# Weights laid out by the host in reading order, gates kept in the tokens' order, and a new order of the work

## The chip, the cores and the metric

The kernel runs on one core of a Trainium2 chip. Such a core has a matrix engine (PE; its weight loads are listed apart as PEld), a vector engine (DVE), a scalar engine (ACT), a GpSimd engine (POOL) and a sync engine (SP), which here issues the DMAs. The metric is the device time of one execution in microseconds (us), as the median of several runs.

## The reference

Two sequences of 512 tokens with 1024 features (`x_prompt`, `x_sample`) pass through the same two layers. Layer 1 is differential attention, layer 2 retention in both directions. Both project to queries, keys, values and a gate of 2048 columns, and multiply the mixer's output by the gate's SiLU before the output projection.

```python
h = rms_norm(x, norm_g[i], NORM_EPS)
proj = h @ w_in                                   # (512, 1024) @ (1024, 8192 or 6144)
q, k, v, gate = jnp.split(proj, [...], axis=-1)
# layer 1: rotary halves; a = softmax(q1 k1) - lam * softmax(q2 k2); o = a @ v
# layer 2: rotation of even and odd columns; retention forward plus backward
o = rms_norm(o, subln_g, SUBLN_EPS)               # layer 1: times 1 - lambda_init
o = o.reshape(B, S, D_INNER) * jax.nn.silu(gate)
x = x + o @ w_out                                 # (512, 2048) @ (2048, 1024)
```

A last `rms_norm` closes the trunk. All of it is float32.

## The kernel before

**Products.** Each float32 operand is split into two parts, a high part (a cast, `hi_of`, line 496, on ACT) and the rest (a subtraction, `lo_of`, line 499, on DVE), and a product takes three passes on PE (`PASSES`). A projection of 256 columns is a `Unit`: its 1024 x 256 block of weights is loaded as two tiles of 512 KB (`raw`, four buffers), split into `ws` tiles (seven buffers), and multiplied by a scheme of seven half-size products, P1 to P7, in place of eight. Sums of weight blocks (line 667, `st` tiles) and sums of the transposed input (line 573, `m` tiles, split into `b` tiles by lines 496 and 499) feed them; products come out in the banks `pj`, `sc` and `o` (`tp` serves transposes), and `evac` copies a bank to a `c` tile on ACT (line 775) or adds a bank and a `c` tile into an `e` tile on DVE (line 783). There are four `c` and eight `e` buffers.

**The token order.** PE reads the input with tokens woven (tokens a and a + 256 side by side), so outputs of a unit come out in woven order. A gate unit (`gate_done`) takes the tanh (line 879, into the `c` tile that its sum has used up), forms (1 + tanh) x (line 886, into the `e` tile; for the first head line 882, in two halves, which puts the tokens in order), scales it (line 888) and stores it to DRAM (`g`, 256 KB). Weights of wide units (values) and of the output projection are woven while they are split: the two instructions read and write a 128 x 1024 tile in steps of two elements.

**Later use.** `load_sg` loads the gate again, and `weigh` (line 969) multiplies the mixer's output by it into another `c` tile, `og`, reading the woven gate in steps of two. `og` is split (lines 496, 499), and the sum of its squares is transposed (line 982) for the norm.

**What sets the order.** `Plan.op` records every operation with a cost and its predecessors, `arrange` places the operations on the engines by a list schedule in order of due times, and `issue` then adds random shifts to the due times of operations near the times in the table `SHIFTS` (time, span back, size, share, seed), a row at a time. The result is one fixed program per engine, each engine working strictly in its own order. All loads and stores go through SP's queue (line 492) in the program's order. A tile can be written again only when the last reader or store of its buffer is done. In this program the last use of a gate's `c` buffer is line 886 and that of its `e` buffer is the store.

Of the kernel before, what the change touches and what calls it, by code (L numbers as in the profile page):

```python
# [13 lines left out]
ALU = mybir.AluOpType  # L14
# [68 lines left out]
def unwoven_rows(t):  # L83
    return t.rearrange("p k (b a) -> p k a b", a=2)


def flat_unwoven_rows(t):
    return t.rearrange("p k (a b) -> p k a b", a=2)


class Buf:
# [22 lines left out]
    (11.25, 30, 4, 0.5, 330243),  # L114
    (621.17, 30, 0.3, 0.5, 683747),
    (617.17, 30, 4, 1, 573989),
    (9.22, 4, 0.3, 0.5, 209685),
    (983.72, 4, 1, 0.5, 4667),
    (619.77, 4, 2, 0.5, 822278),
    (981.05, 4, 4, 0.5, 73582),  # L120
    (993.13, 30, 2, 1, 330152),
    (38.58, 16, 2, 1, 882644),
    (992.0, 4, 4, 1, 27528),
    (982.44, 30, 1, 1, 197187),
    (69.81, 8, 4, 1, 506276),
    (71.79, 16, 4, 0.05, 134658),
    (50.47, 30, 2, 0.05, 359379),
    (14.98, 16, 4, 0.2, 753457),
    (10.72, 30, 2, 0.2, 157696),
    (7.22, 8, 2, 0.2, 458750),  # L130
# [201 lines left out]
def trunk_kernel(  # L332
# [289 lines left out]
    class Unit:  # L622
        def __init__(self, w, c0, kind, done, view=None, weave=woven):
# [3 lines left out]
            self.view = view or (lambda r, i: r[:, :, i * P:(i + 1) * P])  # L627
# [8 lines left out]
        def take(self, i, k):  # L636

            if (i, k) not in self.x:
                c0 = self.c0 + (256 * i if self.wide else 0)
                r = slot(self.early + k, [P, 4, 256], F32) if self.early is not None else raw_t([P, 4, 256])  # L640
                src = self.w[k * S:(k + 1) * S, c0:c0 + 256].rearrange("(k p) c -> p k c", p=P)
# [5 lines left out]
                if self.wide:  # L647
                    self.x[i, k] = ((lambda: r.t), r)
                else:
                    for n in range(2):  # L650
                        self.x[n, k] = ((lambda n=n: self.view(r.t, n)), r)
            return self.x[i, k]

        def like(self, t):

            if self.wide or len(self.x[0, 0][0]().shape) == 3:
                return t
            return t.rearrange("p k (j i) -> p k j i", j=2)

        def prep(self, op):  # L660
# [3 lines left out]
            def combine(a, b, fn):  # L664
                t = st_t([P, 4, n])
                out = ((lambda: self.like(t.t)), t)
# [22 lines left out]
            if op == "P1" and self is first_units[0]:  # L689
                for k in range(2):  # L690
                    ks = slice(2 * k, 2 * k + 2)
                    hi_of(2 * n, lambda ks=ks: self.like(hi[0]())[:, ks], lambda ks=ks: src[0]()[:, ks],
                          [(src[1], n) for n in (2 * k, 2 * k + 1)], [(s, (0, k))])
                    lo_of(2 * n, lambda ks=ks: self.like(lo[0]())[:, ks], lambda ks=ks: src[0]()[:, ks],
                          lambda ks=ks: self.like(hi[0]())[:, ks],
# [1084 lines left out]
```

## Time and profile before

| | |
|---|---|
| median of 3 runs | 1723.61 us (1723.57 to 1723.65) |
| the profiled execution | 1725.69 us, with a span of 1723.9 us from the first to the last instruction |
| mean granted clock of PE in the span | 0.999 |
| PE, DVE, ACT, POOL busy | 1709.6, 1500.4, 935.1, 127.9 us |
| bytes moved | 328.82 MB, of it 209.55 MB read from HBM |
| busiest DMA queue (SP's) | 55.7% of 16 engines |

The table's busy times are averages over stages with different limits. A row of the trace gives the start, the duration, the engine, the line of the program, output and input, and in brackets the idle time ahead of it with what ended it. Rows carry the names that the program gives to its tiles: `arena` is one large buffer for inputs, queries, keys and values, `pad` holds small columns.

### The profile page before, as it was taken

The numbers are of one execution on the slowest core, as the hardware profiler recorded it, in microseconds if no ns is written. First come the engines' busy times: TensorE is split into PE (matmuls) and PEld (weight loads), VectorE is DVE, ScalarE is ACT, GpSimd is POOL, SyncE is SP. The second block draws the span as 40 slices with busy tenths as digits, with TensorE's granted clock in tenths as the row PEclk, the third lists the DMA queues.
The fourth block names the chain that finished last, engine by engine and source line by source line (L and its number), as shares of the span: only waits on it lengthen the run. The fifth ranks groups of instructions, "written<-read, shape, count | busy, mean of one in ns | idle before, by whom it ended". The sixth has DMA issues, their size and how long they took to land.

```text
span 1723.9 us, 27813 instructions
## 1 busy us (share of the span) xinstructions
PE 1709.6 (99%) x10317; PEld 1558.3 (90%) x10317; DVE 1500.4 (87%) x2406; ACT 935.1 (54%) x1864; POOL 127.9 (7%) x256
## 2 busy tenths in 40 slices
PE   9999999999999999999999999999999999999998
PEld 7889989999988889999999988898999998999997
DVE  8978888788699889988888898888898977999988
ACT  8754454444444665555555877555545464544446
POOL 1000000000000012111111200000000000111114
PEclk9999999999999999999999999999999999999999
DMA  6345546564545695555454525475747569665652
GB/s 228 127 159 149 172 151 185 173 193 136 186 135 177 225 357 192 196 196 195 160 201 142 196 68 166 138 217 171 225 138 249 156 211 410 255 250 198 247 205 98
DMA packets 162816, 328.82 MB, mean 191 GB/s; under 512 B 12772, under 2 KB 76920, under 8 KB 162680
## 3 DMA queue, kind: packets, MB, share of 16 engines
q1 hardware_dynamic: 162352, 326.71, 55.7%
q8 instruction: 81, 1.33, 0.3%
q14 instruction: 55, 0.45, 0.1%
q10 hardware_dynamic: 328, 0.34, 0.1%
HBM read 209.55 MB, written 117.44 MB: 190 GB/s over the span
## 4 chain that ended last, share of the span: by engine, by line
PE 92%; DVE 4%; ACT 1%; DMA 1%; issue 1%; POOL 0%; SPq 0%; POOLq 0%; DVEq 0%; ACTq 0%
PE pj L722 20%; PE pj L1060 18%; PE sc L722 11%; PE pj L732 10%; PE o L722 8%; PE sc L732 5%; PE o L1395 5%; PE sc L1334 5%; PE o L732 2%; PE o L1605 2%; PE sc L1560 1%; PE tp L1584 1%; PE o L1613 1%; PE pj L1375 1%; PE tp L1375 1%; DVE ws L499 1%
## 5 line engine op out<-in xcount | busy, mean ns | idle before, releaser
L1060 PE MATMUL pj<-ws,arena 128*128 128x512 f32 x1542 | 358.2, 380 | 0.0
L1060 PEld LDWEIGHTS pj<-ws,arena 128*128 128x128 f32 x1542 | 283.9, 189 | 36.2
L722 PE MATMUL pj<-b,ws 128*128 128x512 f32 x1080 | 251.4, 380 | 0.3 <-DVE b L499 0.3
L722 PEld LDWEIGHTS pj<-b,ws 128*128 128x128 f32 x1080 | 202.5, 189 | 28.5 <-DVE b L499 0.7
L1066 DVE SCALAR_TENSOR_TENSOR b<-pj,pad,b 128x512 f32<-128x512 f32 (+1 forms) x257 | 190.6, 743 | 12.4 <-PE pj L1060 11.8
L496 ACT CAST ws<-st 128x512 fp32r<-128x512 f32 (+1 forms) x192 | 140.4, 738 | 101.3 <-PE pj L722 28.5
L499 DVE TENSOR_TENSOR ws<-raw,ws 128x512 fp32r<-128x512 f32 (+2 forms) x165 | 153.2, 932 | 44.8 <-ACT ws L496 42.7
L496 ACT CAST ws<-raw 128x512 fp32r<-128x512 f32 (+2 forms) x165 | 153.6, 936 | 66.9 <-PE o L722 35.4
L499 DVE TENSOR_TENSOR ws<-st,ws 128x512 fp32r<-128x512 f32 (+1 forms) x192 | 151.6, 795 | 39.9 <-ACT ws L496 37.3
L722 PE MATMUL sc<-arena,ws 128*128 128x512 f32 x768 | 176.9, 379 | 0.0
L722 PE MATMUL o<-arena,ws 128*128 128x512 f32 x744 | 169.4, 380 | 0.0
L722 PEld LDWEIGHTS sc<-arena,ws 128*128 128x128 f32 x768 | 144.8, 189 | 20.4
L722 PEld LDWEIGHTS o<-arena,ws 128*128 128x128 f32 x744 | 139.5, 189 | 19.4 <-DVE arena L559 0.3
L722 PE MATMUL pj<-arena,ws 128*128 128x512 f32 x636 | 148.8, 379 | 0.0
L722 PEld LDWEIGHTS pj<-arena,ws 128*128 128x128 f32 x636 | 119.4, 189 | 16.5
L732 PE MATMUL pj<-ws,b 128*128 128x256 f32 x960 | 115.0, 275 | 0.0
L1352 ACT ACTIVATE b<-sc,pad 128x512 f32<-128x512 f32 x128 | 87.3, 691 | 50.8 <-DVE pad L1342 50.7
L775 ACT COPY c<-pj 128x512 f32<-128x512 f32 x104 | 62.0, 597 | 97.0 <-PE pj L722 61.4
L732 PEld LDWEIGHTS pj<-ws,b 128*128 128x128 f32 x960 | 111.7, 192 | 0.4
L1334 PE MATMUL sc<-arena 128*128 128x512 f32 x384 | 96.8, 388 | 0.5 <-ACT b L1352 0.5
L496 ACT CAST os<-e 128x512 fp32r<-128x512 f32 x96 | 66.0, 693 | 57.7 <-DVE e L783 18.2
L1395 PEld LDWEIGHTS o<-arena 128*128 128x128 f32 x768 | 90.7, 192 | 1.7
(234 smaller groups left out, 2886.6 us busy)
## 6 DMA issues: line engine op xcount, KB each, us to landing
qk<-os SPq DMA_DIRECT2D x192, 256.0 KB, 3.6
arena<-qk SPq DMA_DIRECT2D x96, 512.0 KB, 6.6
v<-os SPq DMA_DIRECT2D x64, 512.0 KB, 4.7
arena<-v SPq DMA_DIRECT2D x64, 512.0 KB, 4.1
raw<-in_da_w_in_dram SPq DMA_DIRECT2D x63, 512.0 KB, 4.9
raw<-in_ret_w_in_dram SPq DMA_DIRECT2D x48, 512.0 KB, 5.0
os<-g SPq DMA_DIRECT2D x32, 512.0 KB, 7.3
g<-e SPq DMA_DIRECT2D x45, 256.0 KB, 5.3
```

Source lines behind the costliest of these rows:

```text
L496: act(n, lambda: nc.scalar.copy(dst(), src()), r, w)
L499: dve(n, lambda: nc.vector.tensor_tensor(dst(), src(), hi().bitcast(F32), op=ALU.subtract), r, w)
L722: nc.tensor.matmul(ps.t, a[u][0]()[:, k, :], self.weave(bt[k][:, v, :]), start=(opens and k == 0 and i == 0), stop=(k == 3 and i == 2), sk ...
L732: nc.tensor.matmul(ps[:, (t % 2) * 256:(t % 2) * 256 + 256], bt[k][:, v, t * P:(t + 1) * P], woven(a[u][0]()[:, k, :]), start=(opens and t ...
L775: act(S, lambda c=c, ps=ps: nc.scalar.copy(c.t, ps.t), [ps], [c])
L1060: nc.tensor.matmul(ps[:, here], o[a][:, e, t * P:(t + 1) * P], woven(u[b][:, e, :])[:, p * n // 2:(p + 1) * n // 2, :], start=(m == 0), st ...
L1066: axpy(n, lambda half=half, here=here, ps=ps: nc.vector.scalar_tensor_tensor(half, ps[:, here], rr[:, t % 2:t % 2 + 1], half, op0=ALU.mult ...
L1334: nc.tensor.matmul(s.t, q[:, a, t * P:(t + 1) * P], woven8(k[:, b, :]), start=(n == 0), stop=(n == 2))
L1352: act(840, lambda j=j, s=s, m=m: nc.scalar.activation(p[:, j, :], s.t, AF.Exp, bias=m.t, accum_out=sm[:, 2 * j + n:2 * j + n + 1]), [s, m] ...
L1375: nc.tensor.transpose(tp[:, j * P:(j + 1) * P], p[:, 0, j * P:(j + 1) * P], ident.t)
L1395: nc.tensor.matmul(o[:, e * 256:(e + 1) * 256], v[b][:, j, e * P:(e + 1) * P], woven(aT[a][:, j, :]), start=(n == 0), stop=(n % 12 == 11), ...
L1605: nc.tensor.matmul(o[:, e * 256:(e + 1) * 256], v_[v][:, 2 * c + j, e * P:(e + 1) * P], woven(a_[:, u, j * 256:(j + 1) * 256]), start=(e = ...
```

## The change

The host lays out the four weight matrices. The input weights become blocks of 256 columns, in each of which a partition's 4 x 256 numbers stand together (4 KB in one piece, where the load before gathered pieces of 1 KB); the order of rotary halves, of even and odd columns and the weaving are put in there, so that the two splitting instructions read and write with step one. The output weights become such blocks too (one piece of 4 KB, where it was two of 2 KB).

The gate puts the tokens in order where it is formed: lines 879 and 886 read the bank or the `e` tile in steps of two, for every head but the first, which does it in steps of eight as before. The result now stays in the tile of the tanh (`c`, or `m` for the product that is read from its bank), so that the store reads that tile, and the `e` tile is free after line 886. `weigh` reads the gate in step one. The table of shifts has 20 rows in place of 17. PE's instructions are the same in number and kind up to their order.

```diff
@@ the table of shifts @@
 SHIFTS = (
-    (11.25, 30, 4, 0.5, 330243),
-    (621.17, 30, 0.3, 0.5, 683747),
...
+    (620.76, 30, 1, 0.5, 820808),
+    (7.22, 4, 4, 0.5, 214000),
...
@@ Unit.take @@
-                src = self.w[k * S:(k + 1) * S, c0:c0 + 256].rearrange("(k p) c -> p k c", p=P)
+                src = self.w[c0 // 256, k].rearrange("p (k c) -> p k c", k=4)
...
-                        self.x[n, k] = ((lambda n=n: self.view(r.t, n)), r)
+                        self.x[n, k] = ((lambda n=n: r[:, :, n * P:(n + 1) * P]), r)
@@ Unit.prep @@
-            if self.wide:
-                flat, from_ = flat_unwoven_rows, lambda: unwoven_rows(src[0]())
-            else:
-                flat, from_ = self.like, src[0]
-            hi_of(4 * n, lambda: flat(hi[0]()), from_, [src[1]], [hi[1]])
-            lo_of(4 * n, lambda: flat(lo[0]()), from_, lambda: flat(hi[0]()), [src[1], hi[1]], [lo[1]])
+            hi_of(4 * n, hi[0], src[0], [src[1]], [hi[1]])
+            lo_of(4 * n, lo[0], src[0], hi[0], [src[1], hi[1]], [lo[1]])
@@ gate_done @@
         def done(i, g, tiles, s, psum):
             x = tiles[0]
             th = m_t("th") if psum else s[("c1", "c2")[g] if i == 0 else "c5"][0]
-            out = th if psum or first else x
-            flat, back = (flat_unwoven8, unwoven8) if first else (lambda t: t, lambda t: t)
+            flat, back = (flat_unwoven8, unwoven8) if first else (flat_unwoven, unwoven)
             act(S, lambda: nc.scalar.activation(flat(th.t), back(x.t), AF.Tanh, scale=0.5), [x], [th])
             if first:
                 for a in range(2):
                     dve(256, lambda a=a: nc.vector.scalar_tensor_tensor(
-                        flat(out.t)[:, :, a, :], flat(th.t)[:, :, a, :], 1.0, back(x.t)[:, :, a, :], op0=ALU.add, op1=ALU.mult),
-                        [th, x], [out])
+                        flat(th.t)[:, :, a, :], flat(th.t)[:, :, a, :], 1.0, back(x.t)[:, :, a, :], op0=ALU.add, op1=ALU.mult),
+                        [th, x], [th])
             else:
-                dve(S, lambda: nc.vector.scalar_tensor_tensor(out.t, th.t, 1.0, x.t, op0=ALU.add, op1=ALU.mult),
-                    [th, x], [out])
-            act(S + 120, lambda: nc.scalar.activation(out.t, out.t, AF.Copy, scale=gcol[:, gc + i:gc + i + 1]),
-                [out, gcol], [out])
-            dma(lambda: dst[g][:, i, :], lambda: out.t, [out], [(dst[g], i)], 256)
+                dve(S, lambda: nc.vector.scalar_tensor_tensor(
+                    flat(th.t), flat(th.t), 1.0, back(x.t), op0=ALU.add, op1=ALU.mult), [th, x], [th])
+            act(S + 120, lambda: nc.scalar.activation(th.t, th.t, AF.Copy, scale=gcol[:, gc + i:gc + i + 1]),
+                [th, gcol], [th])
+            dma(lambda: dst[g][:, i, :], lambda: th.t, [th], [(dst[g], i)], 256)
         return done
@@ weigh @@
         dve(S, lambda: nc.vector.tensor_tensor(
-            flat_halved(og.t), own(y.t), part_of(sg, c).rearrange("p e (a b) -> p e a b", a=2), op=ALU.mult), [y, sg], [og])
+            flat_halved(og.t), own(y.t), sg[:, :, here].rearrange("p e (a b) -> p e a b", a=2), op=ALU.mult), [y, sg], [og])
@@ out_weights @@
-        src = w[h * 256:(h + 1) * 256, i * S:(i + 1) * S].rearrange("(e p) c -> p e c", p=P)
+        src = w[h, i].rearrange("p (e c) -> p e c", e=2)
         dma(lambda: r.t, lambda: src, [], [r], 512)
         hi, lo = ws_t([P, 2, S]), ws_t([P, 2, S])
-        hi_of(1024, lambda: flat_unwoven_rows(hi.t), lambda: unwoven_rows(r.t), [r], [hi])
-        lo_of(1024, lambda: flat_unwoven_rows(lo.t), lambda: unwoven_rows(r.t), lambda: flat_unwoven_rows(hi.t),
-              [r, hi], [lo])
+        hi_of(1024, lambda: hi.t, lambda: r.t, [r], [hi])
+        lo_of(1024, lambda: lo.t, lambda: r.t, lambda: hi.t, [r, hi], [lo])
@@ on the host @@
+def _laid(inputs):
+    import numpy as np
+    def weave(a):
+        return a.reshape(*a.shape[:-1], -1, 2).swapaxes(-1, -2).reshape(a.shape)
+    def blocks(w, turns):
+        w = np.asarray(w)[0].reshape(2, 4, P, -1, 256)
+        out = []
+        for n in range(w.shape[3]):
+            out.append(turns(n)(w[:, :, :, n]).transpose(0, 2, 1, 3).reshape(2, P, 4 * 256))
+        return np.ascontiguousarray(np.stack(out))
+    def halves(a):
+        return a.reshape(*a.shape[:-1], 2, 2, 64).swapaxes(-2, -3).reshape(a.shape)
+    def parities(a):
+        return np.moveaxis(a.reshape(*a.shape[:-1], 2, 64, 2), -1, -3).reshape(a.shape)
+    def outs(w):
+        w = weave(np.asarray(w)[0].reshape(NH, 2, P, 2, S))
+        return np.ascontiguousarray(w.transpose(0, 3, 2, 1, 4).reshape(NH, 2, P, 2 * S))
+    def kind(first, second):
+        return lambda n: first if n < second // 256 else weave if n < (second + DI) // 256 else lambda a: a
+    return dict(da_w_in=blocks(inputs["da_w_in"], kind(halves, 2 * DI)),
+                ret_w_in=blocks(inputs["ret_w_in"], kind(parities, 2 * D)),
+                da_w_out=outs(inputs["da_w_out"]), ret_w_out=outs(inputs["ret_w_out"]))
```

Three places of the two programs follow, without the numbers of the rows. Line numbers differ between them: 492 is now 487 (DMA), 499 is 494 (the rest of a split), 573 is 568, 743 is 727, 783 is 767, 882 is 865, 1230 is 1199, 1257 is 1226.

PE near its first product, about 14 us into the program; the first names the bank and the tiles read, `b` being rows of the normed input and `ident` the identity for transposes. Before:

```order
L1230 MATMUL sc_248<-ident_240,b_259 128x128
L743 MATMUL pj_355<-arena,ws_73 128x256 x6
L1230 MATMUL tp_298<-ident_240,b_243 128x128
L1230 MATMUL tp_298<-ident_240,b_252 128x128
L1230 MATMUL tp_298<-ident_240,b_255 128x128
L1230 MATMUL tp_298<-ident_240,b_259 128x128
L1257 MATMUL sc_327<-ident_240,b_259 128x128 x2
```

After:

```order
L1226 MATMUL o_325<-ident_240,b_255 128x128 x2
L1226 MATMUL sc_322<-ident_240,b_259 128x128 x2
L1226 MATMUL o_325<-ident_240,b_259 128x128 x2
L727 MATMUL pj_350<-arena,ws_73 128x256 x6
L1199 MATMUL sc_248<-ident_240,b_244 128x128
L1199 MATMUL sc_248<-ident_240,b_252 128x128
```

The first product (the rows with `ws`) stood ahead of the four transposes of line 1230 into `tp` and of the last of line 1257, and behind four of line 1230 into `sc`; now it stands behind all of line 1257 and ahead of all of line 1230.

DVE up to the last split that the first stage of products waits for, at about 72 us; the last of these splits is the row `b` from `m` ahead of the final row. Before:

```order
L573 TENSOR_TENSOR m_466<-m_466,os_601 128x512
L783 TENSOR_TENSOR e_517<-o_330,c_497 128x512
L783 TENSOR_TENSOR e_543<-pj_355,c_520 128x512
L499 TENSOR_TENSOR b_866<-m_466,b_866 128x512
L573 TENSOR_TENSOR m_434<-m_434,e_580 128x512
L882 SCALAR_TENSOR_TENSOR c_520<-c_520,e_543 128x64x4
L573 TENSOR_TENSOR m_427<-m_427,e_565 128x512
L882 SCALAR_TENSOR_TENSOR c_520<-c_520,e_543 128x64x4
L499 TENSOR_TENSOR b_886<-m_434,b_886 128x512
L499 TENSOR_TENSOR b_890<-m_427,b_890 128x512
L783 TENSOR_TENSOR e_558<-pj_394,c_527 128x512
```

After:

```order
L767 TENSOR_TENSOR e_537<-pj_350,c_471 128x512
L494 TENSOR_TENSOR ws_85<-st_487,ws_85 128x512
L568 TENSOR_TENSOR m_461<-m_461,os_592 128x512
L865 SCALAR_TENSOR_TENSOR c_471<-c_471,e_537 128x64x4
L568 TENSOR_TENSOR m_457<-m_457,e_575 128x512
L494 TENSOR_TENSOR b_885<-m_461,b_885 128x512
L865 SCALAR_TENSOR_TENSOR c_471<-c_471,e_537 128x64x4
L494 TENSOR_TENSOR b_889<-m_457,b_889 128x512
L494 TENSOR_TENSOR b_826<-m_455,b_826 128x512
L767 TENSOR_TENSOR e_557<-pj_379,c_534 128x512
```

An evacuation of line 783 has left this stretch, a weight's split (`ws` from `st`) has come in, and one split of line 494 now stands between the two half-instructions of the first gate. The last two splits stand together at the end in both.

SP between 1414 and 1427 us, from the stores of the last gates (`g`) to the second output weight of layer 2 (`raw` from `in_ret_w_out_dram`). Before:

```order
L492 DMA g_191<-e_245 128x512
L492 DMA arena<-kt_198 128x2x512
L492 DMA arena<-qk_152 128x1024
L492 DMA g_191<-e_517 128x512
L492 DMA arena<-qk_153 128x1024
L492 DMA arena<-v_154 128x1024 x2
L492 DMA arena<-kt_199 128x2x512
L492 DMA arena<-qk_156 128x1024
L492 DMA arena<-qk_157 128x1024
L492 DMA raw_264<-in_ret_w_out_dram 128x2x512
L492 DMA g_195<-e_543 128x512
```

After:

```order
L487 DMA g_191<-c_594 128x512
L487 DMA os_389<-g_151 128x1024
L487 DMA g_191<-c_468 128x512
L487 DMA arena<-kt_198 128x2x512
L487 DMA arena<-qk_152 128x1024
L487 DMA arena<-qk_153 128x1024
L487 DMA arena<-v_154 128x1024 x2
L487 DMA arena<-kt_199 128x2x512
L487 DMA arena<-qk_156 128x1024
L487 DMA arena<-qk_157 128x1024
L487 DMA raw_264<-in_ret_w_out_dram 128x1024
L487 DMA g_195<-c_471 128x512
```

The second of the two stores of `g_191` stands ahead of the keys' and queries' loads and no longer between them; both are read from `c` tiles. The weight's load is still ahead of the next gate's store.

## Rows read from the trace of the kernel before

**Rows 1.** Busy time of each engine over the whole span (the page's first part).
```profile
PE 1709.6 (99%) x10317; PEld 1558.3 (90%) x10317; DVE 1500.4 (87%) x2406; ACT 935.1 (54%) x1864; POOL 127.9 (7%) x256
```

**Rows 2.** Stretches: us, busy us per engine (count), PE clock, DMA share, GB/s.
```profile
10.00:20.00 10.00, 8.54 (x56) 6.86 (x56) 10.00 (x25) 10.00 (x25) 0.54 (x1) 1.00 1.05 380
20.00:73.00 53.00, 52.16 (x256) 45.16 (x254) 52.52 (x94) 40.21 (x72) 3.66 (x4) 1.00 0.33 109
73.00:600.00 527.00, 526.95 (x3092) 480.14 (x3093) 446.59 (x683) 255.04 (x402) 0.00 (x0) 1.00 0.54 170
600.00:620.00 20.00, 19.32 (x110) 16.92 (x109) 18.08 (x34) 15.54 (x37) 0.39 (x2) 1.00 0.94 368
620.00:1420.00 800.00, 799.91 (x4920) 733.29 (x4919) 699.64 (x1118) 455.49 (x939) 68.07 (x162) 1.00 0.54 184
1000.00:1040.00 40.00, 40.00 (x193) 35.13 (x191) 40.00 (x67) 27.33 (x48) 0.00 (x0) 1.00 0.26 86
1420.00:1460.00 40.00, 38.32 (x246) 35.06 (x245) 28.43 (x48) 20.18 (x43) 2.32 (x4) 1.00 1.03 404
1460.00:1700.00 240.00, 239.92 (x1537) 220.71 (x1535) 223.74 (x365) 113.30 (x285) 35.67 (x57) 1.00 0.58 217
```

**Rows 3.** Waits of PE: what waited, for whom: total us, times, longest.
```profile
PE tp L982 <- DVE b L499: 1.7, 2, 1.4
PE sc L1334 <- ACT b L1352: 0.5, 1, 0.5
```

**Rows 4.** Timeline of the two waits before 73 us: start, duration, instruction.
```profile
43.05 0.33 PE L1230 MATMUL tp<-ident,b 128*128 128x128 f32 x1 [0.52 <-DVE arena L559]
...
71.71 1.28 DVE L499 TENSOR_TENSOR b<-m,b 128x512 fp32r<-128x512 f32 x2
...
73.05 0.48 PE L722 MATMUL pj<-b,ws 128*128 128x512 f32 x1 [0.34 <-DVE b L499]
```

**Rows 5.** Timeline of SP, ACT, DVE and PE from 1415 to 1443 us.
```profile
1415.50 0.70 ACT L888 ACTIVATE e<-e,pad 128x512 f32<-128x512 f32 x1
...
1423.21 0.58 ACT L775 COPY c<-pj 128x512 f32<-128x512 f32 x1 [1.01 <-PE pj L722]
...
1426.52 0.38 SPq L492 DMA_DIRECT2D raw<-in_ret_w_out_dram  x1
...
1437.62 1.45 ACT L496 CAST ws<-raw 128x1024 fp32r<-128x1024 f32 x1 [1.84 <-DMA raw<-in_ret_w_out_dram]
1439.09 1.34 DVE L499 TENSOR_TENSOR ws<-raw,ws 128x1024 fp32r<-128x1024 f32 x1 [1.96 <-ACT ws L496]
...
1440.35 0.75 DVE L969 TENSOR_TENSOR c<-e,os 128x512 f32<-128x512 f32 x1
...
1443.02 0.44 PE L982 MATMUL tp<-ident,m 128*128 128x128 f32 x2 [1.45 <-DVE b L499]
```

**Rows 6.** Groups by form: instruction, count, busy us, mean ns, idle before.
```profile
L496 ACT CAST ws<-raw 128x1024 fp32r<-128x1024 f32 x56 | 81.8, 1461 | 3.8 <-DMA raw<-in_ret_w_out_dram 3.8
L499 DVE TENSOR_TENSOR ws<-raw,ws 128x1024 fp32r<-128x1024 f32 x56 | 76.5, 1366 | 28.9 <-ACT ws L496 28.2
L667 DVE TENSOR_TENSOR st<-raw,raw 128x1024 f32<-128x1024 f32 x16 | 19.6, 1223 | 0.0
L969 DVE TENSOR_TENSOR c<-e,os 128x512 f32<-128x512 f32 x32 | 26.5, 827 | 0.0
L969 DVE TENSOR_TENSOR c<-o,os 128x512 f32<-128x512 f32 x32 | 22.2, 694 | 21.6 <-PE o L1395 21.5
L1216 ACT ACTIVATE arena<-b 128x1024 fp32r<-128x1024 f32 x6 | 6.6, 1120 | 0.0
```

**Rows 7.** DMA issues from 1410 to 1450 us: count, size, median us to landing.
```profile
g<-e SPq DMA_DIRECT2D x5, 256.0 KB, 8.8
...
v<-os SPq DMA_DIRECT2D x1, 512.0 KB, 11.1
```

**Rows 8.** DMA issues over the whole span, the first head's gates.
```profile
g<-c SPq DMA_DIRECT2D x3, 256.0 KB, 2.9
```

More of the change, by code (lines that the diff above doesn't have):

```diff
@@ L80, in flat_unwoven8 @@
     return t.rearrange("p (c a b) -> p c a b", a=2, b=4)
[L83 to L88, printed above, removed]
 class Buf:
@@ L113 @@
 SHIFTS = (
-    (11.25, 30, 4, 0.5, 330243),
-    (621.17, 30, 0.3, 0.5, 683747),
[L116 to L130, printed above, removed]
+    (620.76, 30, 1, 0.5, 820808),
+    (7.22, 4, 4, 0.5, 214000),
+    (68.05, 8, 2, 0.5, 311094),
+    (619.13, 8, 2, 1, 308539),
+    (619.13, 4, 4, 1, 918764),
+    (564.95, 4, 4, 0.05, 220113),
+    (9.5, 8, 1, 0.2, 393358),
+    (7.47, 16, 4, 0.5, 512845),
+    (619.61, 16, 2, 0.5, 603592),
+    (619.14, 4, 2, 0.5, 704480),
+    (615.14, 8, 2, 1, 456826),
+    (10.22, 16, 1, 1, 682499),
+    (13.06, 16, 2, 1, 486441),
+    (7.95, 30, 0.3, 0.5, 193508),
+    (10.12, 16, 2, 1, 732672),
+    (980.69, 30, 1, 1, 534216),
+    (71.69, 4, 4, 0.2, 663146),
+    (69.59, 30, 1, 0.2, 361338),
+    (56.68, 30, 2, 0.2, 66962),
+    (11.22, 4, 1, 1, 45693),
 )
@@ L622, in trunk_kernel, with __init__ @@
     class Unit:
-        def __init__(self, w, c0, kind, done, view=None, weave=woven):
+        def __init__(self, w, c0, kind, done, weave=woven):
             self.w, self.c0, self.kind, self.done = w, c0, kind, done
-            self.view = view or (lambda r, i: r[:, :, i * P:(i + 1) * P])
             self.wide = kind == "wide"
@@ L650, in take @@
                     for n in range(2):
-                        self.x[n, k] = ((lambda n=n: self.view(r.t, n)), r)
+                        self.x[n, k] = ((lambda n=n: r[:, :, n * P:(n + 1) * P]), r)
             return self.x[i, k]
[L654 to L658, printed above, removed]
         def prep(self, op):
@@ L665, in combine @@
                 t = st_t([P, 4, n])
-                out = ((lambda: self.like(t.t)), t)
+                out = ((lambda: t.t), t)
                 dve(4 * n, lambda: nc.vector.tensor_tensor(out[0](), a[0](), b[0](), op=fn), [a[1], b[1]], [t])
@@ L691, in prep @@
                     ks = slice(2 * k, 2 * k + 2)
-                    hi_of(2 * n, lambda ks=ks: self.like(hi[0]())[:, ks], lambda ks=ks: src[0]()[:, ks],
+                    hi_of(2 * n, lambda ks=ks: hi[0]()[:, ks], lambda ks=ks: src[0]()[:, ks],
                           [(src[1], n) for n in (2 * k, 2 * k + 1)], [(s, (0, k))])
-                    lo_of(2 * n, lambda ks=ks: self.like(lo[0]())[:, ks], lambda ks=ks: src[0]()[:, ks],
-                          lambda ks=ks: self.like(hi[0]())[:, ks],
+                    lo_of(2 * n, lambda ks=ks: lo[0]()[:, ks], lambda ks=ks: src[0]()[:, ks],
+                          lambda ks=ks: hi[0]()[:, ks],
                           [*((src[1], n) for n in (2 * k, 2 * k + 1)), (s, (0, k))], [(s, (1, k))])
@@ L946, in projections @@
             yield
-    def part_of(sg, c):
-        if sg.name == "sg0":
-            return sg[:, :, c * 256:(c + 1) * 256]
-        return unwoven_rows(sg.t)[:, :, c, :]
     def halved(t):
@@ L1011, in load_sg @@
         t = os_t(F32, name)
-        t.name = name
         dma(lambda: t.t, lambda: src[:], [src], [t], 512)
@@ L1120, in trunk_kernel @@
     x_d = {(g, t): dram([P, D], f"x{g}{t}") for g in range(NG) for t in range(NT)}
-    w1, wo1, w2, wo2 = da_w_in[0], da_w_out[0], ret_w_in[0], ret_w_out[0]
-    def half_view(r, i):
-        return r.rearrange("p k (j two i) -> p k j two i", j=2, two=2)[:, :, :, i, :]
-    def parity_view(r, i):
-        return r.rearrange("p k (j i two) -> p k j i two", j=2, two=2)[:, :, :, :, i]
+    w1, wo1, w2, wo2 = da_w_in, da_w_out, ret_w_in, ret_w_out
     def mixed(ropes, gates, wides, n, n_gates):
@@ L1143, in units1 @@
                       rot_done({g: qk_d[0, which, h, g] for g in range(NG)}, tab, which == 0, None,
-                               woven8 if which else woven), half_view, woven8 if which else woven)
+                               woven8 if which else woven), woven8 if which else woven)
                  for h in range(NH) for which in range(2)]
-        gates = [Unit(w1, 3 * DI + h * 256, "pair", gate_done({g: g_d[0, h, g] for g in range(NG)}, 16, h == 0), None,
+        gates = [Unit(w1, 3 * DI + h * 256, "pair", gate_done({g: g_d[0, h, g] for g in range(NG)}, 16, h == 0),
                       woven if h else woven8)
@@ L1156, in units2 @@
                       rot_done({g: qk_d[1, which, h, g] for g in range(NG)}, tab2, which == 1,
-                               (h, kt_d) if which else None), parity_view)
+                               (h, kt_d) if which else None))
                  for h in range(0, NH, 2) for which in (1, 0)]
@@ L1322, in fetch1_v @@
         vt[h, g] = load_v(v_d[0, h, g], 10 + 4 * g, 64)
-        sg[h, g] = load_sg(g_d[0, h, g], "sg" if h else "sg0")
+        sg[h, g] = load_sg(g_d[0, h, g])
     def scores(i):
@@ L1767 @@
     arrays, args = {}, []
-    named = [(n, _np.ascontiguousarray(_np.asarray(inputs[n]))) for n in _INS] + _tables()
+    laid = _laid(inputs)
+    named = [(n, laid[n] if n in laid else _np.ascontiguousarray(_np.asarray(inputs[n]))) for n in _INS] + _tables()
     for name, a in named:
```

## The prediction

> **What bounds the kernel now.** I read the busy times of the whole span first, then the stretches, then what PE waited for, then the timeline around each wait. PE is busy 1709.6 us of 1723.9, DVE 1500.4, ACT 935.1 [rows 1]. An average says little about a stage, so the stretches come next [rows 2]. In three long ones (73 to 600, 620 to 1420 and 1460 to 1700 us) PE is idle for 0.05, 0.09 and 0.08 us in all: no edit can win there, and one can lose only by using up the lead that DVE, ACT and the loads have. PE idles in four short stretches: 10 to 20 us (1.46 us), 20 to 73 (0.84), 600 to 620 (0.68) and 1420 to 1460 (1.68). That is 4.66 us, the most that a better order can take from these stages, as PE's instructions stay the same. The clock is 1.00 in every row, so it carries no term.
>
> Three different engines stand behind the four. Up to 73 us it is DVE: busy 10.00 of 10 and then 52.52 of 53 us [rows 2]. Around 610 us the row of waits shows a chain of softmax steps on ACT (0.5 us) [rows 3]. Around 1441 us PE waits once for 1.45 us for a split on DVE [rows 3, 5], which stands behind an output weight that landed late, while the DMA engines are full (share 1.03) [rows 2].
>
> **The start, to 73 us: 0.** The first product now runs ahead of the transposes of line 1230, and may win a part of the 1.46 us of 10 to 20 us; the wait at 43.05 (0.52 us, for line 559) may go too [rows 2, 4]. But the next wait of PE, at 73.05 us, is for the split that begins at 71.71 (two in one row, 1.28 us) [rows 4]. That split comes when DVE has worked through all that its order puts ahead of it, and from 10 to 73 us DVE has 0.48 us of idle time. What PE wins earlier it waits for at 73 us, unless DVE's list gets shorter. By the two orders an evacuation moves out of the stretch and a weight's split moves in, and the gate's half-instructions stay: I take 0. The gain is at most DVE's idle 0.48 plus one evacuation of some 0.7 us (half of the row of two at 71.71 stands for it), so -1.2. On the other side, the first gates' stores now hold a `c` tile: one wait of DVE or ACT for a store in this stretch would cost up to the 2.9 us of its landing [rows 8].
>
> **73 to 600 us and the long stretches: +0.2.** The splits of the woven weights read in step one. There are 56 on each engine: ACT 1461 ns, DVE 1366 ns [rows 6]. The nearest linear rows with as many elements are line 1216 on ACT, 1120 ns, and line 667 on DVE, 1223 ns [rows 6], which would save 56 x 0.34 = 19 us on ACT and 56 x 0.14 = 8 us on DVE. Line 969 falls from 827 towards 694 ns, the row of the first layer's other half (32 x 0.13 = 4.3 us). Line 886 reads its input in steps of two now; at the same 0.13 us on each, the 60 of them (two layers, eight heads, four results, less the first head's four) take about 8 us back from DVE's gain, and line 879 does so on ACT. DVE's sum thus falls by some 4 us, ACT's by more than 10. All of it lies beside a PE that is idle for 0.22 us in 1567 [rows 2]: worth nothing. Loads in pieces of 4 KB may land sooner, also hidden, at a DMA share of 0.54 to 0.58. The one place where a loss can show is 1000 to 1040 us: DVE is busy 40.00 of 40 us there while PE waits for nothing [rows 2], so a lead is being used up; eight gate instructions of 0.13 us more make 1.0 us. I take +0.2, as PE is at 40.00 too and a lead is there; bounds 0 and +1.0.
>
> The Trainium skill (SBUF — State Buffer, "Door 1: The DMA port swizzle (why `[64,N]` ≈ `[32,N]`)") says that a line of SBUF is 16 bytes and that up to 4 float32 one can stride for free, so that a step of two would cost nothing. By it line 886 would lose nothing and the splits would win nothing; rows 6 speak against it with 1366 against 1223 ns on the same engine, though the two lines also write different types. By that rule the term at 1441 us below would be -0.6 in place of -1.1.
>
> **The softmax chain at 600 to 620 us: 0.** The shifts move DVE instructions here, but the wait is for ACT's exponentials behind a row maximum, which no edit shortens. PE's idle 0.68 us [rows 2] is the bound on the gain. On the other side a split of 1.37 us [rows 6] that moves into the chain would cost half of that, as DVE has 1.92 us idle there: bounds -0.7 and +0.7.
>
> **The output weight at 1441 us: -1.1.** The chain in the timeline [rows 5]: load issued 1426.52, cast from 1437.62 (ACT idle until the landing), its rest from 1439.09, line 969 from 1440.35, and PE goes on at 1443.02. With the durations above the cast ends 0.34 us sooner, the rest 0.14, line 969 about 0.06 (0.75 to the 0.69 of its twin): -0.54. The load itself can come earlier: SP's order has moved a store of the gate ahead of keys and queries, so that eight loads of 512 KB, not seven and a store, stand ahead of it; and its pieces are now 4 KB. With 404 GB/s and full engines, a 256 KB store less in the way is 262144 / 404000 = 0.65 us. I take 0.56 of it, so -1.1 in all. Bounds: all of PE's 1.68 us there [rows 2], and +0.5 where the load is not sooner and the store in another place delays it.
>
> **Sum.** 0 + 0.2 + 0 - 1.1 = -0.9. The profiled execution took 1725.69 us, 2.08 above the median of the runs, 1723.61; the same difference on that scale gives 1722.7 us.
>
> **Rivals.**
> - *All small waits go.* For: the order has been changed at just these places. Against: DVE's full row up to 73 us, where a win of PE turns into a longer wait. It gives 1723.6 - 4.66 = 1718.9 us.
> - *Nothing arrives at PE.* The full DMA engines, not the splits, set 1441 us; a load moved by one place lands no sooner since the bytes ahead are the same, and DVE's order hides the 0.54. For: share 1.03 [rows 2], 11.1 us for a landing nearby [rows 7]. Against: the cast and its rest stand on the path in any case. 1723.6 us.
> - *Slower: `c` tiles held by stores.* Line 775 writes the four `c` buffers, and now each that held a gate is free only when its store has landed, where before it was free after line 886. The place: the copy at 1423.21 us takes the buffer of the gate that line 888 finishes at 1415.50 + 0.70 = 1416.2 [rows 5]; its store is issued no earlier, and a landing took 8.8 us in this stretch [rows 7], so 1425.0: ACT would stand for 1.8 us, with the next gates' tanh and the bank behind it, and for 4.1 us at the 11.1 us of the longest row. Against: PE has three such banks and reads the next one first, and the lead of the copies may cover it; in quiet stretches a landing took 2.9 us [rows 8]. It decides from a landing of 1423.2 - 1416.2 = 7.0 us on. With 4.1 us less the 1.1 won: 1726.6 us.
>
> The Trainium skill (DMA: Bandwidth & Descriptors, "Anatomy of one DMA — SWDGE (gpsimd) path") has a fit of 2.0 us plus the bytes over 436 GB/s for another issuing path: 256 KB would take an estimated 2.6 us, and the store would be down long before 1423 us. Rows 8 agree with 2.9 us, rows 7 with 8.8 do not, as engines are full there; by the fit this rival falls away.
>
> **How the numbers follow.** The measurement tells a change from none at about 0.2%, 3.4 us here. The forecast has a chance of 0.52, all waits gone 0.17, nothing 0.19, held tiles 0.12. Faster by more than 3.4 us (below 1720.2) needs nearly all the waits: the second case, with a little of the first, 0.18. Slower (above 1727.0) needs the third rival with more than one such stop: 0.08. Within: 0.74. The range runs from 1718.8, which holds the second case, to 1726.3, which holds the bounds of the start (+2.9) and most of the held tiles. The forecast's own range is 1720.8 to 1724.2.
>
> **What would show it.** Right: the profile after has the casts of `raw` near 1.12 us and their rest near 1.22, the idle share of PE at 1420 to 1460 us about 0.6, and PE's wait near 72 us longer by what 10 to 45 us won. Wrong: a wait at 73 us that is gone while DVE is still full from 10 to 73 (then DVE's list did get shorter); ACT's line 775 waiting on a DMA with PE waiting behind it; or PE waiting anywhere in the three long stretches.

## The result and the profile after

The changed kernel (after, in what follows) takes 1727.29 us (median of 11 runs, 1726.49 to 1729.60) against 1723.69 us before (11 runs too): a ratio of 1.0022, interval 1.0013 to 1.0032. It is slower by 3.6 us, where 1722.7 was predicted and 1726.3 was the end of the range. One run of 6414 us of the kernel before, and one of 1740.72 us of the layout alone below, leave their medians where they are, but the second widens an interval.

The stretches of after, in the columns of [rows 2]:

```profile
10.00:20.00 10.00, 8.94 (x63) 7.50 (x62) 9.90 (x24) 9.81 (x24) 0.54 (x1) 1.00 1.03 408
20.00:73.00 53.00, 51.43 (x251) 44.00 (x249) 52.95 (x93) 41.75 (x74) 3.03 (x4) 1.00 0.30 103
73.00:600.00 527.00, 526.24 (x3087) 478.95 (x3087) 445.44 (x682) 249.84 (x400) 0.00 (x0) 1.00 0.53 167
600.00:620.00 20.00, 17.91 (x99) 15.84 (x100) 16.35 (x30) 13.71 (x28) 0.39 (x2) 1.00 0.97 377
620.00:1420.00 800.00, 797.42 (x4909) 731.49 (x4909) 689.65 (x1118) 437.75 (x939) 67.61 (x162) 1.00 0.53 184
1420.00:1460.00 40.00, 40.00 (x250) 36.84 (x249) 29.25 (x50) 24.02 (x52) 2.32 (x4) 1.00 1.00 393
1460.00:1700.00 240.00, 240.00 (x1545) 221.27 (x1544) 217.98 (x365) 106.13 (x281) 32.86 (x57) 1.00 0.60 225
```

PE's idle time in them is 8.06 us, against 4.88 in [rows 2]. It is gone from 1420 us on, and has grown from 20 to 73 (0.84 to 1.57), from 73 to 600 (0.05 to 0.76, of it 0.45 from 590 on), from 600 to 620 (0.68 to 2.09) and from 620 to 1420 (0.09 to 2.58, of it 0.80 at 622 and 1.62 at 996). PE's waits in after name the new ones (columns of [rows 3]):

```profile
PE o L706 <- DVE e L554: 1.6, 1, 1.6
PE sc L1303 <- DMA arena<-qk: 1.5, 1, 1.5
...
PE sc L1303 <- DVE pad L1311: 1.0, 1, 1.0
```

The second and third stand at 601 and 603 us. Both end with the landing of a load of keys or queries: the second with one that was issued at 592.53 and landed at 601.02, the third, which the page puts down to DVE's row maximum, with one that was issued at 594.32 and landed at 602.92. A wait of PEld's just ahead of it is on that load's semaphore and ends at 602.95, while DVE was done at 602.71. Both loads stand in a queue into which a gate's store has moved:

```profile
591.48 0.42 SPq L487 DMA_DIRECT2D g<-c  x1
591.98 0.45 SPq L487 DMA_DIRECT2D qk<-os  x1
592.53 0.89 SPq L487 DMA_DIRECT2D arena<-qk  x1
593.46 0.77 SPq L487 DMA_DIRECT2D qk<-os  x1
594.32 0.56 SPq L487 DMA_DIRECT2D arena<-qk  x1
...
599.31 0.59 ACT L759 COPY c<-pj 128x512 f32<-128x512 f32 x1 [1.71 <-DMA g<-c]
...
601.07 0.92 PE L1303 MATMUL sc<-arena 128*128 128x512 f32 x3 [1.52 <-DMA arena<-qk]
...
603.01 0.89 PE L1303 MATMUL sc<-arena 128*128 128x512 f32 x3 [1.02 <-DVE pad L1311]
```

The first, at 996 us, comes from a power of one column (the middle norm) on POOL, that takes 2.38 us and not its usual 0.54, and on which ACT's scaling waits:

```profile
987.79 0.68 DVE L655 TENSOR_TENSOR st<-st,raw 128x512 f32<-128x512 f32 x1
988.29 2.38 POOL L1079 TENSOR_TENSOR pad<-pad,pad 128x1 f32<-128x1 f32 x1 [2.36 <-ACT pad L1072]
988.39 1.28 DVE L494 TENSOR_TENSOR arena<-m,arena 128x512 fp32r<-128x512 f32 x2
989.59 0.68 DVE L494 TENSOR_TENSOR ws<-raw,ws 128x512 fp32r<-128x512 f32 x1
990.71 1.15 ACT L475 ACTIVATE b<-b,pad 128x1024 f32<-128x1024 f32 x1 [1.53 <-POOL pad L1079]
```

The single durations changed as [rows 6] had bounded them, or more; the groups of after:

```profile
L491 ACT CAST ws<-raw 128x1024 fp32r<-128x1024 f32 x56 | 58.6, 1047 | 1.7 <-DMA raw<-in_ret_w_out_dram 1.6
L494 DVE TENSOR_TENSOR ws<-raw,ws 128x1024 fp32r<-128x1024 f32 x56 | 68.1, 1216 | 24.7 <-ACT ws L491 21.2 <-PE pj L1035 1.7 <-PE pj L706 1.7
L862 ACT ACTIVATE c<-e 128x512 f32<-128x512 f32 x48 | 40.8, 850 | 15.0 <-DVE e L767 14.8
L869 DVE SCALAR_TENSOR_TENSOR c<-c,e 128x512 f32<-128x512 f32 x45 | 37.3, 832 | 5.0 <-ACT c L862 4.5
L946 DVE TENSOR_TENSOR c<-e,os 128x512 f32<-128x512 f32 x32 | 21.8, 682 | 0.0
```

### The profile page after: what moved, and what is told of

The parts are those of the page before. It is cut to its first block, busy times and chain, and to the rows that moved or that the text cites. A ratio compares the mean times of both kernels' runs of the same rounds, so it can differ in the third digit from the quotient of the medians.

```text
span 1726.2 us, 27794 instructions
## 1 busy us (share of the span) xinstructions
PE 1709.5 (99%) x10317; PEld 1558.9 (90%) x10317; DVE 1484.5 (86%) x2405; ACT 909.2 (53%) x1865; POOL 123.8 (7%) x256
## 4 chain that ended last, share of the span: by engine, by line
PE 87%; DVE 7%; ACT 3%; DMA 1%; issue 1%; POOL 0%; SPq 0%; DVEq 0%; POOLq 0%; ACTq 0%
PE pj L706 18%; PE pj L1035 17%; PE sc L706 10%; PE pj L716 10%; PE o L706 5%; PE sc L716 5%; PE o L1364 5%; PE sc L1303 5%; PE o L716 2%; PE o L1574 2%; DVE ws L494 1%; PE o L1582 1%; PE sc L1529 1%; PE tp L1553 1%; ACT c L1068 1%
## 5 line engine op out<-in xcount | busy, mean ns | idle before, releaser
L491 ACT CAST ws<-st 128x512 fp32r<-128x512 f32 (+1 forms) x192 | 132.4, 694 | 114.6 <-DVE st L655 28.1
L494 DVE TENSOR_TENSOR ws<-raw,ws 128x512 fp32r<-128x512 f32 (+2 forms) x165 | 141.9, 864 | 41.2 <-ACT ws L491 32.8
L491 ACT CAST ws<-raw 128x512 fp32r<-128x512 f32 (+2 forms) x165 | 124.8, 762 | 68.6 <-PE o L706 38.1
```

The source lines that it names most:

```text
L491: act(n, lambda: nc.scalar.copy(dst(), src()), r, w)
L494: dve(n, lambda: nc.vector.tensor_tensor(dst(), src(), hi().bitcast(F32), op=ALU.subtract), r, w)
```

## The experiments

Every kernel below was timed beside the kernel before, which stood between 1723.48 and 1723.88 us.

**A second profile of the kernel before.**

> The kernel before once more, for a second profile: its first profiled execution took 2.1 us more than the median of its runs. If the waits of PE at 1441 us and from 668 to 850 us belong to the kernel, they stand here too, at the same sizes within 0.3 us, and the 2.1 us lie at the start or the end; if they vary, the layout's gain in the traces is partly chance.

One run, 1723.24 us, span 1721.4. The wait at 1441 us is not in it:

```profile
1420.00:1460.00 40.00, 39.77 (x255) 36.54 (x254) 30.26 (x52) 21.48 (x49) 3.35 (x6) 1.00 1.03 403
```

PE idles 0.23 us there, not 1.68 [rows 2], while the waits at 43, 73 and 610 us return at their sizes. Set side by side by the starts of the same PE instructions, the first profile runs 0.3 to 0.4 us behind the second until 1420 us, 2.1 us behind from 1440 us on and 2.5 at the end. So 1.7 of the 2.5 us between the two lie in that one place, and from 620 to 1420 us they run alike. Over the same seven stretches this trace has 3.22 us of idle PE; after has 4.84 more, and its span is 4.8 us longer (1726.2 against 1721.4). So the loss is PE's waiting, and the rows of after account for it.

**The layout alone.** Host layout and loads as changed, everything else as before, with each engine's order to the letter:

```diff
-src = self.w[k * S:(k + 1) * S, c0:c0 + 256].rearrange("(k p) c -> p k c", p=P)
+src = self.w[c0 // 256, k].rearrange("p (k c) -> p k c", k=4)
...
-flat, from_ = flat_unwoven_rows, lambda: unwoven_rows(src[0]())
+flat, from_ = (lambda t: t), src[0]
```

> The kernel before with the host's layout of the weights alone: loads in pieces of 4 KB, splits in step one; the gate and the order of every engine are those of before. Theory A (the change is slower because gates hold c tiles until their stores land around 600 us, and because a power on POOL stands behind DVE near 990 us, not because of the layout): 1722.5 to 1723.6 us, the split of raw on DVE near 1.22 us and its cast near 1.05 us, PE's wait at 1441 us shorter by 0.5 us or more. Theory B (the layout itself shifts loads and splits so that something is late): 1725 us or more, with a new wait of PE in one of the long stretches.

1721.66 us against 1723.74, below even A's range. The interval of the ratio is 0.998 to 1.002, so that this run alone does not settle the sign. It shows no cost of the layout, and B falls.

**Pieces of 4 KB alone.** Loads from blocks as above, but `_laid` leaves the columns in their order, and the splits go in steps of two as before.

```diff
+def blocks(w):
+    w = np.asarray(w)[0].reshape(2, 4, P, -1, 256)
+    return np.ascontiguousarray(np.stack([w[:, :, :, n].transpose(0, 2, 1, 3).reshape(2, P, 4 * 256)
+                                          for n in range(w.shape[3])]))
...
```

> The kernel before with the weights in blocks, so that loads read pieces of 4 KB, but with the columns in their own order, so that casts and splits of wide and output weights still go in steps of two; orders as before. Theory H (the layout's gain of 2.0 us comes from the shorter splits: POOL stands behind the 1.37 us split of DVE in each head, and casts at 1450 and 1690 us are shorter): 1723.2 to 1723.7 us, and POOL's 1.38 us stays. Rival (it comes from the loads): 1721.7 to 1722.4 us.

1723.23 us, ratio 0.9997 (0.9988 to 1.0006): the same as before. By the medians 1.6 of the 2.0 us come with the step-one splits, or 1.4 if each kernel is set against the kernel before beside it. Theory H's time is met. Its casts near 1450 and 1690 us do win, but its path through POOL does not: POOL's scalar ends sooner, and nothing of that reaches PE. Before, in the head at 654 us:

```profile
654.46 1.37 DVE L499 TENSOR_TENSOR ws<-raw,ws 128x1024 fp32r<-128x1024 f32 x1
654.64 1.38 POOL L1362 TENSOR_SCALAR pad<-pad,pad 128x1 f32<-128x1 f32 x1 [2.89 <-DVE pad L1361]
...
656.05 0.75 DVE L1364 SCALAR_TENSOR_TENSOR b<-b,pad 128x512 f32<-128x512 f32 x1 [0.23 <-POOL pad L1362]
...
657.44 0.60 PE L1375 MATMUL tp<-ident,b 128*128 128x128 f32 x4
```

With the layout alone:

```profile
654.18 1.20 DVE L499 TENSOR_TENSOR ws<-raw,ws 128x1024 fp32r<-128x1024 f32 x1
654.36 1.24 POOL L1361 TENSOR_SCALAR pad<-pad,pad 128x1 f32<-128x1 f32 x1 [2.89 <-DVE pad L1360]
...
657.17 0.60 PE L1374 MATMUL tp<-ident,b 128*128 128x128 f32 x4
```

POOL's scalar ends 0.14 us sooner with DVE's split, and DVE's next step waits for it, but the head's transposes on PE start 2.98 and 2.99 us after the split began: no sooner. Where the time is won shows when pieces alone and the layout alone are set side by side by the starts of the same PE instructions. They run level until 640 us; then the layout alone wins 1.1 us from 660 to 900 us, 0.4 at 1446 and 0.4 at 1698, where PE no longer waits 0.2 us at line 982; the spans differ by 1.7 us in the end. The 1.1 us come almost whole in five heads, 0.2 us in each, where ACT's cast is what counts. Before, in the first of the five:

```profile
701.51 1.55 ACT L496 CAST ws<-raw 128x1024 fp32r<-128x1024 f32 x1
...
702.94 0.71 ACT L1352 ACTIVATE b<-sc,pad 128x512 f32<-128x512 f32 x1
...
703.79 0.51 PEld L1334 LDWEIGHTS sc<-arena 128*128 128x128 f32 x3 [0.31 <-ACT b L1352]
703.79 1.58 PE L1334 MATMUL sc<-arena 128*128 128x512 f32 x6
```

With the layout alone:

```profile
701.11 1.04 ACT L496 CAST ws<-raw 128x1024 fp32r<-128x1024 f32 x1
...
702.05 0.70 ACT L1351 ACTIVATE b<-sc,pad 128x512 f32<-128x512 f32 x1
...
703.11 1.27 PEld L1333 LDWEIGHTS sc<-arena 128*128 128x128 f32 x6
703.33 1.46 PE L1333 MATMUL sc<-arena 128*128 128x512 f32 x6
```

The exponential (line 1352) follows the cast in ACT's queue, and a weight load of PE waits for it; with the shorter cast it waits for nothing. PE's own row shows no idle time for this wait: its matmuls are only drawn longer, 1.58 us for six and not 1.46.

**The changed kernel without the waits for its stores.** The order of after; `c` and `e` tiles share their twelve places, and each takes the one free for longest:

```diff
-self.tile = self.make(self.nth % self.bufs)
+self.tile = self.make(self.nth % self.bufs if self.place is None else self.place)
...
+b.place = min(range(12), key=lambda i: until[i])
```

> The changed kernel in its own order, but each c and e tile takes the place, of the twelve of both kinds together, that has been free for longest; nothing else differs. Theory A: ACT's copy at 599.3 us, which waited 1.71 us for the store of a gate, waits for none; PE's waits at 599 to 602 us (1.5 and 1.0 us) shrink by 1.7 us or more: 1723.9 to 1725.6 us. Theory C (the new place of the stores and loads in SP's queue makes the keys late, whoever holds a tile): PE still waits 1.5 us for the load of queries or keys, and the time stays at 1726.5 to 1727.5 us.

1727.37 us, ratio 1.0023 (1.0013 to 1.0032). ACT waits for no store of a `c` tile any more, and PE's waits at 599 to 603 us stay at 1.4 and 1.0 us. The held tile's wait is real, and taking it away wins nothing: theory A falls at this place, C stands.

**Two loads and one store in SP's queue.** The kernel just told, with three DMAs moved at 590 us. The numbers are those of the program's operations: 1898 is the gate's store, 1917 and 1919 are the loads of the second keys, and each is put right behind the operation named second, as far as its dependences allow:

```diff
+for n, after in [(1898, 1922), (1917, 1918), (1919, 1917)]:
...
+    out.insert(at, item)
```

> The changed kernel in its own order with c and e tiles in the places free for longest, and SP's queue changed at 590 us alone: the gate's store that stood ahead of four loads of queries and keys goes behind them, and the two loads of the second keys go up by one place each. Theory D (what the held c tile costs is the place of its stores in SP's queue: PE waits at 599 us for a load that is late by one store and the store's wait): PE's waits of 1.4 and 1.0 us at 599 to 603 us shrink to under 0.8 us in all, 1725.5 us. Rival E (the DMA engines are full from 590 us on, and what one load wins another loses): PE waits as long at 599 us or soon after, 1726.5 to 1727.5 us.

1724.79 us, ratio 1.0006 (0.9997 to 1.0015). From 590 to 605 us, in after and then here:

```profile
590.00:605.00 15.00, 12.46 (x57) 10.31 (x56) 10.64 (x18) 8.03 (x15) 0.00 (x0) 1.00 0.97 342
```

```profile
590.00:605.00 15.00, 14.61 (x70) 12.48 (x69) 12.39 (x22) 9.25 (x18) 0.00 (x0) 1.00 0.99 350
```

PE's idle time falls from 2.54 to 0.39 us while the DMA engines stay full: what one load wins, no other loses in time to matter. The two loads that PE waited for land at 598.16 and 600.01 us, 2.9 us sooner than in after, where 0.4 us of that is a lead that this run has at 589 us already. In the trace the store goes further back than the expectation says, behind nine loads and two stores, to 601.09. D stands, E falls; how much the store did and how much the two loads, the run does not separate.

**The power on POOL: another form beside it.**

```diff
-dve(n, lambda: nc.vector.tensor_tensor(dst(), src(), hi().bitcast(F32), op=ALU.subtract), r, w)
...
+nc.vector.scalar_tensor_tensor(dst(), src(), 1.0, hi().bitcast(F32), op0=ALU.mult, op1=ALU.subtract)
...
```

> The changed kernel in its own order, with the five DVE subtractions beside the last power on POOL of the middle norm (988 us) written as scalar_tensor_tensor (times 1.0, less the high part) in place of tensor_tensor. Theory A (POOL stands while DVE runs tensor_tensor from two inputs in SBUF): the power takes about 0.55 us in place of 2.38, ACT's scaling no longer waits 1.5 us for it, PE's wait of 1.6 us at 994 to 996 us goes: 1725.6 us. Rival (the power waits for something else): it stays at 2.4 us, and the time at 1727.3 us.

1726.92 us, ratio 1.0020 (1.0012 to 1.0029), and the power as long as ever:

```profile
988.50 2.38 POOL L1087 TENSOR_TENSOR pad<-pad,pad 128x1 f32<-128x1 f32 x1 [2.37 <-ACT pad L1080]
```

So it is not the form. Both forms read two operands from SBUF.

**The power on POOL: DVE held back.**

```diff
...
 nc.gpsimd.tensor_tensor(r.t, ss.t, mhalf[:, 0:1], op=ALU.pow)
+nc.vector.tensor_copy(held.t, r.t)
```

> The changed kernel with one small copy on DVE that waits for the last power of the middle norm on POOL (988 us), ahead of the three subtractions that ran beside it. Theory A (POOL stands while DVE works on two operands from SBUF, in either form of instruction): the power takes 0.55 us in place of 2.38, PE's wait of 1.6 us near 995 us shrinks by 1.3 us or more, 1725.8 us. Rival: the power still takes 2.4 us, 1727.3 us.

1725.19 us (eleven runs from 1724.19 to 1729.54), ratio 1.0012 (1.0003 to 1.0021):

```profile
989.39 0.57 POOL L1084 TENSOR_TENSOR pad<-pad,pad 128x1 f32<-128x1 f32 x1 [2.37 <-ACT pad L1073]
989.99 0.16 DVE L1085 COPY pad<-pad 128x1 f32<-128x1 f32 x1 [0.44 <-POOL pad L1084]
990.07 1.28 DVE L494 TENSOR_TENSOR arena<-m,arena 128x512 fp32r<-128x512 f32 x2
```

0.57 us for the power, and PE's wait of 1.6 us is gone: DVE waits 0.44 us to win 1.8 for POOL. Theory A stands here, in its wider wording.

**Both mends.** The edits of the loads in SP's queue and of the copy on DVE together.

> The changed kernel with both mends: the loads and the gate's store at 590 us in SP's queue, and DVE waiting for the last power on POOL at 988 us. If the two losses stand apart, their gains add: 1727.3 less 2.5 less 2.1 gives 1722.7 us. If they share one cause (PE later anyway, or one slack), the sum is smaller: 1724 us or more.

1723.42 us, ratio 0.9996 (0.9987 to 1.0005): 3.9 of the 4.6 us that the two give singly, between the two cases of the expectation. Most of the two losses stand apart.

**The old table of shifts; the gate back in the `e` tile.** Both have an order of their own.

```diff
-    (620.76, 30, 1, 0.5, 820808),
+    (11.25, 30, 4, 0.5, 330243),
...
-act(..., lambda: nc.scalar.activation(th.t, th.t, AF.Copy, scale=...), [th, gcol], [th])
+act(..., lambda: nc.scalar.activation(out.t, th.t, AF.Copy, scale=...), [th, gcol], [out])
```

> The changed kernel with the kernel before's table of 17 shifts, so layout and held gates are as changed and the order comes out another way. Theory A (held tiles cost 2 to 4 us around 600 us in any order, the power on POOL is a matter of this one order): 1725 to 1727 us, with ACT's copies to c waiting for stores around 600 us, and no power of 2.4 us. Theory C (the searched order is what costs): 1723 to 1724 us.

> The changed layout and the gate in the tokens' order, but the scaled gate goes back into the e tile, so that no c tile waits for a store, with the kernel before's table of shifts: all engines in nearly the order of before. Theory D (held c tiles drive the order that costs): 1721.5 to 1722.5 us, as with the layout alone. Rival (the gate's strided reads on ACT and DVE cost): 1723.5 us or more, with waits of PE on DVE or ACT at 600 or 1440 us.

1727.82 us, ratio 1.0024 (1.0015 to 1.0033), and 1728.57 us, ratio 1.0026 (1.0015 to 1.0037). The first lies above the ranges of both its theories, though ACT's copies do wait for stores (2.4 us in all) and no power takes 2.4 us, as A had it. The second, with no tile held by a store, is the slower of the two: PE idles 3.32 us from 20 to 73 us in it. Theory D, that held tiles drive the cost, falls, and so does the idea that the old table brings back the old order: the same 17 rows, laid over another set of dependences, give another program. The rival's time is met in the second run, but not by its cause, as the next run shows.

**The gate's new form in the old order.** Layout as changed, gate in the tokens' order, scaled into the `e` tile, every engine's order as before: the recorded reads and writes stay those of before, and the calls are new. The other edits are left out here.

```diff
-dve(S, lambda: nc.vector.scalar_tensor_tensor(out.t, th.t, 1.0, x.t, op0=ALU.add, op1=ALU.mult), [th, x], [out])
+dve(S, lambda: nc.vector.scalar_tensor_tensor(flat(th.t), flat(th.t), 1.0, back(x.t), op0=ALU.add, op1=ALU.mult), [th, x], [out])
```

> The layout alone (1721.7 us) with the gate put in the tokens' order as well, every engine's order kept to the letter; the scaled gate goes into the e tile, and c and e tiles take the places free for longest. Theory F (the gate's new form costs nothing by itself, the price of the change is the order): 1721.4 to 1722.2 us. Rival G (strided reads, 0.14 us more on DVE and 0.22 on ACT for each of 45 to 48, come out on PE where DVE is full, up to 73 us and from 980 to 1040): 1722.6 us or more.

1722.14 us, ratio 0.9991 (0.9982 to 1.0000): F. The strided reads, 0.14 us on DVE and 0.22 on ACT each, cost some 0.5 us beside the median of the layout alone.

**Order and computation apart.** First all that the change computes, in the order of before; then what before computes, in the order of after, by recording the reads and writes of the one and calling the other:

```diff
-dma(lambda: dst[g][:, i, :], lambda: out.t, [out], [(dst[g], i)], 256)
+dma(lambda: dst[g][:, i, :], lambda: th.t, [out], [(dst[g], i)], 256)
```

```diff
-dma(lambda: dst[g][:, i, :], lambda: out.t, [out], [(dst[g], i)], 256)
+dma(lambda: dst[g][:, i, :], lambda: out.t, [th], [(dst[g], i)], 256)
```

> All that the change computes (layout, gate in the tokens' order and left in the tanh's tile, stores from there), in the order of the kernel before on every engine; c and e tiles take the places free for longest. Theory F (only the order costs): 1721.7 to 1722.6 us. Rival J (tiles that wait for stores cost by themselves): ACT's copies to c tiles wait for stores, PE waits near 600 or 1440 us, 1724 us or more.

> All that the kernel before computes (its layout, woven gates, scaled gates in the e tile), in the order of the changed kernel on every engine; c and e tiles take the places free for longest. Theory F (only the order costs, 5 us beside the computation): 1723.7 + 5.1 = 1728.8 us, with PE's waits at 599 and 995 us. Rival J (the order is good for what it was made for, the computation costs): 1725 us or less.

| us | order of before | changed order |
|---|---|---|
| computation of before | 1723.48 | 1729.25 |
| changed computation | 1722.20 | 1727.29 |

Ratios to before 0.9992 (0.9983 to 1.0001) and 1.0033 (1.0020 to 1.0045). The order costs 5.8 and 5.1 us, the computation wins 1.3 and 2.0 by the medians: the two add up to within 0.7 us, and the order has its price whatever is computed. That the computation wins is not settled by these intervals alone. The two new kernels share the places of `c` and `e` tiles, which the kernel before and after do not; in the changed order that made no difference (1727.37 against 1727.29). In the first of the two ACT waits for no store of a gate, so J has nothing to stand on there, and its time falls in both; `c` places in turn were not tried in the order of before.

**DVE's list up to 73 us.** The layout alone, with two scalings moved to ACT in their places.

```diff
-fn(e)
+fn("ACT" if n in moved else e)
...
```

> The layout alone with the last two scalings of the first norm that DVE did (0.47 us each, at 24 to 30 us) on ACT at the same places. Theory I (up to 73 us DVE's list alone sets when PE goes on, so whatever shortens it arrives): PE's waits at 42 and 72 us shrink by up to 0.9 us together, 1720.8 us. Rival (ACT, at 9.1 us busy of 10 from 20 to 30 us, is as full, and what it does later costs as much): 1721.6 us or more.

1721.80 us, ratio 0.9987 (0.9978 to 0.9996): beside 1721.66 no gain, and PE's wait for line 559 near 42 us grew from 0.5 to 0.9 us. I falls. It is still the clearest of the versions that beat both kernels.

## Why the prediction was wrong

- **The start (0).** Right in its mechanism, and nearly in size: PE's idle time falls by 0.40 us from 10 to 20 us and grows by 0.73 from 20 to 73, where DVE is busy 52.95 of 53 us. What was won was handed back, and some 0.3 us more. One profile is thin ground for this (the second of the kernel before has the 1.06 us of after from 10 to 20), but seven in each order agree: 1.05 to 1.66 us idle from 10 to 20 in the order of before and 0.58 to 1.06 in the changed one, 0.84 to 1.13 and 1.57 to 1.98 from 20 to 73. It was handed back at 46 and 62 us (0.90 and 0.57), not at 73 as the prediction said. That DVE's list alone sets it was too simple: 0.94 us less of it, taken over by ACT, won nothing.
- **The long stretches (+0.2, "worth nothing").** Wrong on both sides. The shorter splits were not hidden: some 1.6 us arrived. Of these 1.1 us came from 660 to 900 us, where ACT's cast stands ahead of an exponential that PE's weight loads wait for. PE idle for 0.09 us from 620 to 1420 did not mean that nothing could be won there, as this wait stands in PEld's row and not in PE's. And the loss that was looked for as DVE's lead from 1000 to 1040 us came 10 us earlier, through POOL: 2.1 us by the experiment. The working read DVE's and ACT's queues and never POOL's. The trace of before had a sign of it: a scalar that takes 0.34 us elsewhere on POOL takes 1.38 beside DVE's split, at 654.64. The Trainium skill (SBUF — State Buffer, "Who interferes with whom") has the rule that was not weighed: a DVE instruction with two inputs in SBUF contends with a GpSimd instruction that reads SBUF, and the one that comes second waits. The runs agree, with 2.38 us beside either form of the subtraction and 0.57 us without one.
- **The softmax chain at 600 us (0, at most +0.7).** This is the step that failed most: 2.5 us by the experiment. It took the wait for one of ACT's exponentials and asked what moved on DVE. What moved that mattered was SP's queue, a gate's store and two loads of keys, where the DMA engines are full (0.94) [rows 2]: PE then waited 1.52 and 1.02 us for two landings. The orders of that queue were compared at 1414 us alone.
- **The output weight at 1441 us (-1.1).** The whole wait went in after, and little was won by it, as the kernel before has 1.68 us of it in one profile and 0.23 in the other, whose 1723.24 us is the one near the median. The 2.08 us between the profiled execution and the median were put down as a constant difference between two scales; of the 2.5 us between the two profiles 1.7 are that wait. The splits' part of the term arrived nearly in size, 0.4 us for 0.54 (layout alone against pieces alone); that the earlier load won its 0.56, no run shows.
- **The slower rival** had tiles held by stores. Its mechanism shows (ACT waited 1.71 us at 599 us), and taking it away changed nothing. The time came near its 1726.6, which lies outside the range itself, by another cause.
- **A rival that was missing:** that the new order itself is worse. The searched order is 5 us slower for either computation, and no rival but the held tiles had the change slower.

What stays open is what the three moved DMAs at 590 us are worth singly, and how the last 1.2 us between both mends (1723.42) and the changed computation in the old order (1722.20) divide; of the idle time of PE, 1.1 us more stand from 20 to 73 us in the first (1.97 against 0.86) and 1.1 from 590 to 630 (1.79 against 0.67), less what the first wins ahead of 20 us.

## What to carry to other kernels

Before a term rests on a wait, see whether the profiled execution is as fast as the median; if it is slower by about that wait, take a second profile. When an order changes, read every queue at the places where its engine or the DMA is full, SP's and POOL's too, since three DMAs cost 2.5 us and one tiny instruction 2.1 us here by their places. A PE whose row shows no idle time was waiting in its weight loads here: look at PEld's waits too, and set two profiles of one order side by side instruction by instruction. Try the new computation in the old order first: it tells in one run whether order or computation has the price.

## What the runs showed that was not expected

POOL got no turn between four DVE subtractions in a row: its power, 0.54 us in the kernel before, stood from 988.29 to 990.67 us, 0.4 us past the end of that row (990.27). ACT's tanh over an `e` tile read in steps of two and written in two halves went from 633 to 850 ns, the sum on DVE from 688 to 832, while the same two from a bank stayed (595 to 589, 681 to 689).
